# Three buffers of 16 rows, and loads and stores in two parts of every second partition

## The chip, the cores and the metric

The kernel runs on one core of a Trainium2 chip. The metric is device time in microseconds (us), lower is better. A time is the median of the timed executions. The profiled executions give, beside the time, a trace and its span from the first to the last recorded work; the time lies above the span of the same execution (318.93 against 317.3 for the kernel before).

## The reference

Each of 16,384 rows of 1,024 float32 is divided by the sum of its absolute values:

```python
batch, seq, dim = 32, 512, 1024
sums = np.sum(np.abs(x), axis=-1, keepdims=True)
return (x / (sums + 1e-8)).astype(np.float32)
```

67.11 MB have to come in and 67.11 MB have to go out, whatever the kernel does.

## The kernel before

128 partitions (P) take 128 rows at a time in float32. Four buffers hold 12 such rows each, a run of 48 KiB per partition. One DMA loads a buffer, DVE (the vector engine) sums and multiplies, ACT (the scalar engine) multiplies one row (five in the first tile, none in the last four), one DMA stores it. The last tile has 8 rows.

```python
R = 12
BUFS = 4
...
with tc.manual_schedule():
    for i, k in enumerate(rows):          # 12, 12, ..., 12, 8
        x_tile = sbuf.tile([P, R, d], FP32)
        nc.sync.dma_start(out=x_tile[:, :k, :], in_=piece(x_flat, i))
        if i == 0:
            normalize(x_tile, 0, k, k - 5)
        else:
            normalize(x_tile, 0, k, k - 1 if i + BUFS < len(rows) else k)
        nc.scalar.dma_start(out=piece(out_flat, i), in_=x_tile[:, :k, :])
```

`normalize` is a `tensor_reduce` (sum of absolute values), an add of EPS, a reciprocal and a `tensor_mul` on DVE, and for the rows left over a scaled copy each on ACT.

Of the kernel before, what the change touches and what calls it, by code (L numbers as in the profile page):

```python
# [1 line left out]

# [4 lines left out]

FP32 = mybir.dt.float32
EPS = 1e-8


@with_exitstack
def kernel(
    ctx: ExitStack,
    tc: tile.TileContext,
    x: bass.AP,
    out: bass.AP,
):
    nc = tc.nc
    P = nc.NUM_PARTITIONS  # L20

    x_flat = x.flatten_outer_dims()
    out_flat = out.flatten_outer_dims()
    n, d = x_flat.shape




    R = 12
    BUFS = 4  # L30
    HEAD = 32
    per_partition = n // P
    assert n % P == 0 and (per_partition - HEAD) % R == 0
    rows = [R] * ((per_partition - HEAD) // R + 2) + [HEAD - 2 * R]

    def piece(flat, i):
        head = flat[: P * HEAD, :].rearrange("(p r) d -> p r d", p=P)
        if i < 2:
            return head[:, R * i : R * (i + 1), :]
        if i == len(rows) - 1:  # L40
            return head[:, 2 * R :, :]
        a = P * (HEAD + R * (i - 2))
        return flat[a : a + P * R, :].rearrange("(p r) d -> p r d", p=P)

    sbuf = ctx.enter_context(tc.tile_pool(name="sbuf", bufs=BUFS))
    stats = ctx.enter_context(tc.tile_pool(name="stats", bufs=4))

    def normalize(x_tile, r0, k, kv):

        s = stats.tile([P, R], FP32)  # L50
        nc.vector.tensor_reduce(  # L51
            out=s[:, :k],
            in_=x_tile[:, r0 : r0 + k, :],
            axis=mybir.AxisListType.X,
            op=mybir.AluOpType.add,
            apply_absolute_value=True,
        )
        nc.vector.tensor_scalar_add(out=s[:, :k], in0=s[:, :k], scalar1=EPS)  # L58
        inv = stats.tile([P, R], FP32)
        nc.vector.reciprocal(out=inv[:, :k], in_=s[:, :k])  # L60
        nc.vector.tensor_mul(  # L61
            out=x_tile[:, r0 : r0 + kv, :],
            in0=x_tile[:, r0 : r0 + kv, :],
            in1=inv[:, :kv].unsqueeze(2).to_broadcast([P, kv, d]),
        )
        for r in range(kv, k):
            row = x_tile[:, r0 + r, :]
            nc.scalar.activation(  # L68
                out=row,
                in_=row,  # L70
                func=mybir.ActivationFunctionType.Copy,
                scale=inv[:, r : r + 1],
            )

    with tc.manual_schedule():
        for i, k in enumerate(rows):
            x_tile = sbuf.tile([P, R, d], FP32)
            nc.sync.dma_start(out=x_tile[:, :k, :], in_=piece(x_flat, i))  # L78


            if i == 0:
                normalize(x_tile, 0, k, k - 5)
            else:
                normalize(x_tile, 0, k, k - 1 if i + BUFS < len(rows) else k)
            nc.scalar.dma_start(out=piece(out_flat, i), in_=x_tile[:, :k, :])  # L85


# [1 line left out]
_INS = ['x']  # L89
_OUTS = [((32, 512, 1024), 'float32')]  # L90


# [23 lines left out]
```

## Time and profile before

| | before |
|---|---|
| time, median of 3 | 317.25 us (317.13 to 317.62) |
| the profiled execution: time, span | 318.93 us, 317.3 us |
| DVE busy | 268.7 us (85%) |
| ACT busy | 13.5 us (4%) |
| the two DMA queues, share of 16 engines | 49.6% and 48.9% |

The queues' shares add to 98.5%.

### The profile page before, as it was taken

What the parts mean: (1) busy time and instruction counts of PE and PEld (TensorE: products, weight loads), DVE (VectorE), ACT (ScalarE), POOL (GpSimd) and SP (SyncE); (2) the same over time, 40 slices, a digit from 0 to 9 for tenths busy, and PEclk for the clock granted to TensorE, in tenths of its full rate; (3) what the DMA queues carried; (4) which work ended last, traced back from release to release, by engine and by line L of the source; (5) the groups of instructions that cost most, each with busy time, mean ns of one, the idle gap of its engine ahead of it and who ended that gap; (6) DMA issues with size and microseconds to landing.
All of it is one profiled execution on the core that took longest, in us unless ns stands there. A gap on an engine that the chain in (4) does not pass through costs nothing.

```text
span 317.3 us, 170 instructions
## 1 busy us (share of the span) xinstructions
DVE 268.7 (85%) x44; ACT 13.5 (4%) x12; POOL 0.2 (0%) x4
## 2 busy tenths in 40 slices
DVE  0079999999999999989995996799699969999920
ACT  0010601001000000100100010000000000000000
POOL 0000000000000000000000000000000000000000
DMA  8999999999999999999999999999999999999994
GB/s 328 465 397 471 421 378 415 415 465 409 459 434 397 477 415 415 465 409 459 428 403 477 409 428 452 409 471 415 403 477 415 428 430 452 397 477 415 403 425 215
DMA packets 3168, 134.22 MB, mean 423 GB/s; under 512 B 352, under 2 KB 352, under 8 KB 352
## 3 DMA queue, kind: packets, MB, share of 16 engines
q1 hardware_dynamic: 1584, 67.11, 49.6%
q10 hardware_dynamic: 1584, 67.11, 48.9%
HBM read 67.11 MB, written 67.11 MB: 423 GB/s over the span
## 4 chain that ended last, share of the span: by engine, by line
DVE 52%; DMA 34%; another core or an unknown queue 9%; issue 0%; SPq 0%; DVEq 0%; ACTq 0%
DVE s L51 27%; DVE x_tile L61 24%; DMA x_tile<-in_x_dram 18%; DMA out_dram<-x_tile 16%; DVE inv L60 1%; DVE s L58 0%; SPq L78 0%; DVEq L60 0%; ACTq L85 0%
## 5 line engine op out<-in xcount | busy, mean ns | idle before, releaser
L51 DVE TENSOR_REDUCE s<-x_tile 128x12 f32<-128x12288 f32 (+1 forms) x11 | 138.2, 12561 | 32.9 <-DMA x_tile<-in_x_dram 32.9
L61 DVE TENSOR_TENSOR x_tile<-x_tile,inv 128x11264 f32<-128x11264 f32 (+3 forms) x11 | 126.5, 11504 | 0.4
L68 ACT ACTIVATE x_tile<-x_tile,inv 128x1024 f32<-128x1024 f32 x11 | 12.2, 1142 | 153.6 <-DVE inv L60 153.6
L60 DVE RECIPROCAL inv<-s 128x12 f32<-128x12 f32 (+1 forms) x11 | 2.5, 226 | 0.9
L58 DVE TENSOR_SCALAR s<-s 128x12 f32<-128x12 f32 (+1 forms) x11 | 1.9, 173 | 0.4
L68 ACT ACT_TABLE_LOAD x1 | 1.3, 1283 | 17.8 <-DMA x_tile<-in_x_dram 17.8
L100 POOL MEMSET const-bfloat16-1.0<- 128x1 bf16 x1 | 0.1, 102 | 0.0
L100 POOL MEMSET const-uint8-127<- 128x1 uint8 x1 | 0.1, 102 | 0.0
L100 POOL MEMSET const-float32-0.0<- 128x1 f32 x1 | 0.1, 99 | 0.2 <-issue 0.2
L100 POOL MEMSET const-float32-1.0<- 128x1 f32 x1 | 0.1, 99 | 0.0
## 6 DMA issues: line engine op xcount, KB each, us to landing
x_tile<-in_x_dram SPq DMA_DIRECT2D x10, 6144.0 KB, 39.2
out_dram<-x_tile ACTq DMA_DIRECT2D x10, 6144.0 KB, 43.7
x_tile<-in_x_dram SPq DMA_DIRECT2D x1, 4096.0 KB, 35.4
out_dram<-x_tile ACTq DMA_DIRECT2D x1, 4096.0 KB, 13.0
```

The source lines that it names most:

```text
L51: nc.vector.tensor_reduce(out=s[:, :k], in_=x_tile[:, r0 : r0 + k, :], axis=mybir.AxisListType.X, op=mybir.AluOpType.add, apply_absolute_v ...
L58: nc.vector.tensor_scalar_add(out=s[:, :k], in0=s[:, :k], scalar1=EPS)
L60: nc.vector.reciprocal(out=inv[:, :k], in_=s[:, :k])
L61: nc.vector.tensor_mul(out=x_tile[:, r0 : r0 + kv, :], in0=x_tile[:, r0 : r0 + kv, :], in1=inv[:, :kv].unsqueeze(2).to_broadcast([P, kv, d]),)
L68: nc.scalar.activation(out=row, in_=row, func=mybir.ActivationFunctionType.Copy, scale=inv[:, r : r + 1],)
L100: nc = _bacc.Bacc("TRN2", target_bir_lowering=False, num_devices=1)
```

## The change

Its intent is to keep the engines fed with fewer, larger tiles: 3 x 16 rows use the same 48 rows of memory, and splitting each transfer by partition parity lets the even partitions of a buffer be loaded while its odd ones are still stored. DVE gives rows to ACT, and the last tile is finished in two halves of rows. The diff is abridged:

```diff
-    R = 12
-    BUFS = 4
+    R = 16
+    BUFS = 3
+    PARTS = 2
 ...
+        for r in range(k - ka, k):          # ka rows are summed by ACT
+            nc.scalar.activation(out=junk[:, :], in_=rows[:, r, :],
+                func=mybir.ActivationFunctionType.Abs, accum_out=s[:, r : r + 1])
 ...
-            nc.sync.dma_start(out=x_tile[:, :k, :], in_=piece(x_flat, i))
+            for j in range(PARTS):
+                nc.sync.dma_start(
+                    out=x_tile[j::PARTS, :, :], in_=piece(x_flat, i)[j::PARTS, :, :])
+            if i + 1 < tiles:
+                if i == 0:
+                    normalize(x_tile, 5, 6)      # rows summed, multiplied by ACT
+                else:
+                    normalize(x_tile, 0, 3)
+                for j in range(PARTS):
+                    nc.scalar.dma_start(
+                        out=piece(out_flat, i)[j::PARTS, :, :], in_=x_tile[j::PARTS, :, :])
+            else:
+                for h in (slice(0, R // 2), slice(R // 2, R)):
+                    normalize(x_tile[:, h, :], 3, 4)
+                    nc.scalar.dma_start(out=piece(out_flat, i)[:, h, :], in_=x_tile[:, h, :])
```

More of the change, by code (lines that the diff above doesn't have):

```diff
@@ L24, with normalize @@
     n, d = x_flat.shape
-    R = 12
-    BUFS = 4
-    HEAD = 32
-    per_partition = n // P
-    assert n % P == 0 and (per_partition - HEAD) % R == 0
-    rows = [R] * ((per_partition - HEAD) // R + 2) + [HEAD - 2 * R]
-    def piece(flat, i):
-        head = flat[: P * HEAD, :].rearrange("(p r) d -> p r d", p=P)
-        if i < 2:
-            return head[:, R * i : R * (i + 1), :]
-        if i == len(rows) - 1:
-            return head[:, 2 * R :, :]
-        a = P * (HEAD + R * (i - 2))
+    R = 16
+    BUFS = 3
+    PARTS = 2
+    tiles = n // (P * R)
+    assert n == P * R * tiles
+    def piece(flat, i):
+        a = P * R * i
         return flat[a : a + P * R, :].rearrange("(p r) d -> p r d", p=P)
-    sbuf = ctx.enter_context(tc.tile_pool(name="sbuf", bufs=BUFS))
+    sbuf = ctx.enter_context(tc.tile_pool(name="sbuf", bufs=1))
     stats = ctx.enter_context(tc.tile_pool(name="stats", bufs=4))
-    def normalize(x_tile, r0, k, kv):
+    psum = ctx.enter_context(
+        tc.tile_pool(name="psum", bufs=1, space=bass.MemoryType.PSUM)
+    )
+    junk = psum.tile([P, d], FP32)
+    buffers = [sbuf.tile([P, R, d], FP32, name=f"x{b}") for b in range(BUFS)]
+    def normalize(rows, ka, km):
+        k = rows.shape[1]
         s = stats.tile([P, R], FP32)
         nc.vector.tensor_reduce(
-            out=s[:, :k],
-            in_=x_tile[:, r0 : r0 + k, :],
+            out=s[:, : k - ka],
+            in_=rows[:, : k - ka, :],
             axis=mybir.AxisListType.X,
@@ L57, in normalize @@
         )
+        for r in range(k - ka, k):
+            nc.scalar.activation(
+                out=junk[:, :],
+                in_=rows[:, r, :],
+                func=mybir.ActivationFunctionType.Abs,
+                accum_out=s[:, r : r + 1],
+            )
         nc.vector.tensor_scalar_add(out=s[:, :k], in0=s[:, :k], scalar1=EPS)
@@ L61, in normalize @@
         nc.vector.tensor_mul(
-            out=x_tile[:, r0 : r0 + kv, :],
-            in0=x_tile[:, r0 : r0 + kv, :],
-            in1=inv[:, :kv].unsqueeze(2).to_broadcast([P, kv, d]),
-        )
-        for r in range(kv, k):
-            row = x_tile[:, r0 + r, :]
+            out=rows[:, : k - km, :],
+            in0=rows[:, : k - km, :],
+            in1=inv[:, : k - km].unsqueeze(2).to_broadcast([P, k - km, d]),
+        )
+        for r in range(k - km, k):
             nc.scalar.activation(
-                out=row,
-                in_=row,
+                out=rows[:, r, :],
+                in_=rows[:, r, :],
                 func=mybir.ActivationFunctionType.Copy,
@@ L75 @@
     with tc.manual_schedule():
-        for i, k in enumerate(rows):
-            x_tile = sbuf.tile([P, R, d], FP32)
-            nc.sync.dma_start(out=x_tile[:, :k, :], in_=piece(x_flat, i))
-            if i == 0:
-                normalize(x_tile, 0, k, k - 5)
-            else:
-                normalize(x_tile, 0, k, k - 1 if i + BUFS < len(rows) else k)
-            nc.scalar.dma_start(out=piece(out_flat, i), in_=x_tile[:, :k, :])
+        for i in range(tiles):
+            x_tile = buffers[i % BUFS]
+            for j in range(PARTS):
+                nc.sync.dma_start(
+                    out=x_tile[j::PARTS, :, :], in_=piece(x_flat, i)[j::PARTS, :, :]
+                )
+            if i + 1 < tiles:
[5 more added lines that the diff above has]
+                    nc.scalar.dma_start(
+                        out=piece(out_flat, i)[j::PARTS, :, :],
+                        in_=x_tile[j::PARTS, :, :],
+                    )
+            else:
+                for h in (slice(0, R // 2), slice(R // 2, R)):
+                    normalize(x_tile[:, h, :], 3, 4)
+                    nc.scalar.dma_start(
+                        out=piece(out_flat, i)[:, h, :], in_=x_tile[:, h, :]
+                    )
 _INS = ['x']
```

## The prediction

> **What bounds the kernel now.** I began with the busy line and the memory lines of the page. The memory lines carry 67.11 MB in and 67.11 MB out, and the two queues together keep the 16 DMA engines at work 98.5% of the span.
>
> ```profile
> span 317.3 us, 170 instructions
> ...
> DVE 268.7 (85%) x44; ACT 13.5 (4%) x12; POOL 0.2 (0%) x4
> ...
> q1 hardware_dynamic: 1584, 67.11, 49.6%
> q10 hardware_dynamic: 1584, 67.11, 48.9%
> HBM read 67.11 MB, written 67.11 MB: 423 GB/s over the span
> ```
>
> The reader is to see two engines near their limit, DVE at 85% and DMA at 98.5%, and only one of them can be the bound. So next I read the busy time by stretches, with the core's DMA share and GB/s in the last two columns.
>
> ```profile
> 0.00:20.00 20.00, 2.25 (x1) 1.28 (x1) 0.20 (x4) 1.00 0.94 393
> 20.00:40.00 20.00, 19.90 (x5) 5.30 (x5) 0.00 (x0) 1.00 1.00 433
> ...
> 160.00:180.00 20.00, 16.28 (x2) 0.00 (x0) 0.00 (x0) 1.00 1.00 433
> 180.00:200.00 20.00, 15.52 (x5) 1.15 (x1) 0.00 (x0) 1.00 1.00 433
> ...
> 300.00:308.00 8.00, 3.17 (x1) 0.00 (x0) 0.00 (x0) 1.00 0.89 381
> 308.00:317.30 9.30, 0.00 (x0) 0.00 (x0) 0.00 (x0) 1.00 0.56 240
> ```
>
> The rate is the same 433 GB/s where DVE is full (20 to 40 us) and where it rests a fifth of the time (160 to 200 us). The fourteen 20-us stretches from 20 to 300 us lie between 413 and 437 and average 432.6. A share of 1.00 with DVE idle says that the transfers are the bound, and the waits agree: DVE waits for loads, and the load queue waits for stores to free a buffer.
>
> ```profile
> DVE s L51 <- DMA x_tile<-in_x_dram: 32.9, 6, 17.8
> ...
> SPq L78 <- DMA out_dram<-x_tile: 227.0, 7, 55.5
> ```
>
> 17.8 of those 32.9 us are the first load; the other 15.1 us are five waits of 1.1 to 4.3 us between 140 and 259 us. The chain of waits gives DVE 52%, but it runs back along an engine that had slack, so I don't take that share for a bound.
>
> The account of the span follows: 134.22 MB at 432.6 GB/s is 310.3 us. The first 20 us run at 393, which loses (432.6 - 393) x 20 / 432.6 = 1.8 us. From 300 to 308 us it is 381, a loss of 0.95 us: the last multiply ends at 294.48 + 8.69 = 303.17, and the store before the last has about drained by then (the stretch 303 to 304 us has a share of 0.23). From 308 to the end it is 240, a loss of 4.1 us, in which the last packets end unevenly and the last write is confirmed. Sum 310.3 + 1.8 + 0.95 + 4.1 = 317.2.
>
> [...]
>
> **The change part by part.**
> *Bytes:* none removed, none added. The floor of 310.3 us stays. The transfers become 16 loads of 4.19 MB, 14 such stores and two last ones, 32 instead of 22. They queue behind one another, so their issue (0.33 us each on the queue) lies beside transfers already running. A partition's run grows from 48 to 64 KiB; at an unchanged rate I book nothing for it.
>
> *DVE:* a reduce of 12 rows is 12.95 us and of 8 rows 8.68, so 1.07 a row; the multiply of 11 rows is 11.89 and of 7 rows 7.63, also 1.07 a row. The two small operations with their gaps are 0.5 us (30.70 to 31.21). Tile 0: 11 rows reduced 11.9 + 0.5 + 10 rows multiplied 10.8 = 23.2 us. Tiles 1 to 6: 16 rows 17.2 + 0.5 + 13 rows 14.0 = 31.7 us each. Last tile, two halves of 5.5 + 0.5 + 4.4 = 10.4 us. Sum 23.2 + 190.2 + 20.8 = 234 us, 34 us less than 268.7. All of it comes off an engine that isn't the bound, so I value it at nothing in the middle.
>
> *ACT:* 43 row operations instead of 11. At 1.15 us each that is about 50 us, never over 7 us in a row, against 11 to 14 us of DVE beside it (in the last tile 3 x 1.15 and 4 x 1.15 beside 5.5 and 4.4, so at most a few tenths stick out). I take a row sum by ACT to cost what a row copy does.
>
> *Buffers:* 3 x 16 and 4 x 12 are both 48 rows, so as much is loaded before the first store as before: 25.2 MB. Does either queue ever run dry? Tile 0 (8.39 MB) is there at 2 + 8.39 / 0.4326 = about 22 us, normalised at 22 + 23.2 = 45, when 18.8 MB are loaded and 6.4 are left. From then loads and stores share the engines, 216 GB/s each, 19.4 us for a half-buffer transfer. The first half-store lands at 65, with 6.4 - 4.2 = 2.2 MB of loads still queued (10 us of work), and then the next load is released. Every later half repeats this with period 19.4, so loads don't run dry. Stores of tile i are through at about 46 + 38.8 (i + 1); tile 3 is loaded at 114 and normalised at 146, while the stores before it last until 163, a margin of 17 us that repeats because 31.7 is below 38.8. So neither queue runs dry in the middle. Even if a half had to wait for both stores of its buffer, the engines would work off the other queue meanwhile.
>
> *The end:* at 45 us, 67.1 - 18.8 = 48.3 MB are left to load; at 216 GB/s that takes 223 us, so the last load lands near 269. By then 48.3 MB are stored and 18.8 are left, 43 us at full rate. The last tile's halves are ready at 279 and 290. The backlog ahead of them, 18.8 - 8.4 = 10.4 MB, lasts 24 us, until 293. So the last store joins a queue still busy, by some 3 us, and the 0.95 us lost at 300 to 308 us before should go.
>
> *Sum:* 310.3 + 1.8 + 4.1 = 316.2, and as the third loss may return in part or longer runs may save a few tenths, **316.0 us**.
>
> **The rivals.** (1) **Strided halves slow the engines down.** [...] Against it: loads and stores are mixed most of the time,[...] and the row counts of the change look tuned around transfers at full rate. A rate 5% lower means 310.3 x 1.053 + 5.9 = 333 us[...]. I give it one in ten. (2) **A wait for a buffer takes the place of the finer rotation.** Three buffers must carry load, 31.7 us of compute and store within 3 x 38.8 = 116 us. With undivided transfers that is 38.8 + 31.7 + 38.8 = 109, seven to spare; with halves overlapping, one 19.4 less. The margins above speak against it; it could cost 1 to 4 us if completion of halves came late. (3) **The end gets worse:** if the last load lands over 3 us later than I reckon, the last half-store of 4.19 MB stands alone and the lost microsecond stays, 317 to 319. (4) **A real gain from less compute:** only if DVE were the bound. The stretches with a full DMA share and an idle DVE speak against it, and even a loss-free run is 310.3 us plus start and end, about 313; over 2% faster (below 310.9) would need a rate that the engines never show.
>
> **Range and chances.** 313.8 is the floor with some of the end saved; 320 holds rivals 2 and 3. Faster by over 2%: 0.02. Within 2%: 0.87. Slower: 0.11, nearly all of it rival 1.
>
> **What would show it.** Right: both queues' shares still sum to 98 to 99%, the stretches from 20 to 290 us read 430 to 437 GB/s, DVE falls to about 234 us (75% or less) with longer waits for loads, and no dip before the last store. Wrong: a rate under 425 in the load-only first 45 us (rival 1), stretches with the share under 0.97 in the middle (rival 2), or a dip between 285 and 310 us (rival 3). The prediction fails most simply if 64 strided partitions are not spread like 128 whole ones.

Cuts are marked in the text above: passages about the DMA engines and the memory that no trace or run of this case shows, among them a limit for the rate, grounds for and against rival 1, and a loss worked out from them. Rival 1, with its one in ten, is the author's estimate: the kernel before has only transfers of 128 partitions, so no trace then on hand showed one of 64. 310.3 + 1.8 + 4.1 = 316.2 us are worked out from the trace of the kernel before. Only the step from there to the 316.0 us given, for longer runs, is a guess; the traces show no such gain (64 KiB in 2.418 us and 48 KiB in 1.815 are both 27.1 GB/s).

## More of the kernel before

The profiled execution is 1.7 us slower than the median of the timed ones. The stretches at its end, one us each, with the DMA share and GB/s in the last two columns, say why:

```profile
312.00:313.00 1.00, 0.00 (x0) 0.00 (x0) 0.00 (x0) 1.00 1.22 524
313.00:314.00 1.00, 0.00 (x0) 0.00 (x0) 0.00 (x0) 1.00 0.23 98
314.00:315.00 1.00, 0.00 (x0) 0.00 (x0) 0.00 (x0) 1.00 0.08 33
```

A packet is counted where it starts, so a share may exceed 1. The reader is to see that after 313 us only a few packets start: 33 GB/s is one 32 KiB packet in a microsecond. Most of the 16 DMA engines (the engines meant from here on, where no other is named) are done; one still works.

## The result, and the profile after

The changed kernel takes 320.46 us (median of 6, 319.21 to 321.20), the kernel before 316.97 us (median of 6, 316.56 to 317.62). The ratio is 1.0106, 95% interval 1.0081 to 1.013. Ratios here are the mean time of one kernel's fast runs over that of the other's in the same rounds, so not quite the ratio of the medians. The change is clear and small, within 2%, and the time is 0.46 us above the predicted range. It went the wrong way: 0.4% faster was expected (316.0 against 317.25), 1.1% slower came.

The page of the changed kernel, its busy and memory lines (q1 carries the loads, q10 the stores):

```profile
span 319.0 us, 211 instructions
...
DVE 233.5 (73%) x36; ACT 48.2 (15%) x55; POOL 0.2 (0%) x4
...
q1 hardware_dynamic: 1280, 67.11, 49.3%
q10 hardware_dynamic: 1408, 67.11, 48.6%
HBM read 67.11 MB, written 67.11 MB: 421 GB/s over the span
```

DVE lost 35 us and the span grew: compute is not what the kernel waits for. Its waits, and its stretches:

```profile
DVE s L52 <- DMA x<-in_x_dram: 58.6, 6, 23.0
```

```profile
0.00:20.00 20.00, 0.00 (x0) 0.00 (x0) 0.20 (x4) 1.00 0.96 400
20.00:40.00 20.00, 16.82 (x4) 11.53 (x16) 0.00 (x0) 1.00 1.01 439
...
240.00:260.00 20.00, 19.90 (x4) 3.23 (x3) 0.00 (x0) 1.00 1.01 436
260.00:280.00 20.00, 11.67 (x5) 5.04 (x8) 0.00 (x0) 1.00 1.03 446
280.00:300.00 20.00, 13.03 (x5) 10.38 (x13) 0.00 (x0) 1.00 0.94 408
300.00:308.00 8.00, 0.00 (x0) 0.00 (x0) 0.00 (x0) 1.00 1.00 430
308.00:319.00 11.00, 0.00 (x0) 0.00 (x0) 0.00 (x0) 1.00 0.48 209
```

The DMA share lies between 0.94 and 1.07 up to 308 us, and the dip of the kernel before (381 GB/s from 300 to 308) has become 430. The scatter of the stretches, 408 to 459 GB/s from 20 to 300 us, is in the counting: the engines start their 64 KiB packets nearly together, and each packet counts where it starts. With the bytes of each packet spread over its duration, every stretch from 20 to 300 us reads 430 to 434, but for 414 from 40 to 60, where the first store begins. What is lost against the kernel before is lost in the last line. The same end in steps of one us:

```profile
312.00:313.00 1.00, 0.00 (x0) 0.00 (x0) 0.00 (x0) 1.00 0.76 328
313.00:314.00 1.00, 0.00 (x0) 0.00 (x0) 0.00 (x0) 1.00 0.23 98
314.00:315.00 1.00, 0.00 (x0) 0.00 (x0) 0.00 (x0) 1.00 0.08 33
315.00:316.00 1.00, 0.00 (x0) 0.00 (x0) 0.00 (x0) 1.00 0.08 33
316.00:317.00 1.00, 0.00 (x0) 0.00 (x0) 0.00 (x0) 1.00 0.08 33
```

For three microseconds one packet starts per microsecond. The transfers are done but for one engine's share.

**Looking at single engines.** No view names the 16 engines, but the trace records each packet with queue, start, duration and size. One engine's packets follow one another with their records meeting to about 4 ns, so I chained them into 16 sequences. Each has 8.39 MB, to better than 0.1, in the first traces of both kernels. Where two engines are in step a packet may land in the wrong sequence (some sums in other traces are off by more, by 0.5 MB in f4), so I use the ends and averages over all 16, and single packets only where the sequences are well apart.

In the changed kernel most sequences end between 313.0 and 313.8 us, two at 314.6 and 314.8, and one at 317.9. In the kernel before most end at 313.8 to 313.9, two at 314.5 and 315.0 and one at 315.9. Nothing is slow about the packets as such: a 64 KiB packet takes 2.418 us and a 48 KiB one 1.815, both 27.1 GB/s. The late engine has single packets that take longer. Here it is beside an ordinary engine, at the border between two loads (queue: L load, S store; start us, duration ns, bytes; the packets of 4 bytes come at the end of a transfer, 16 to each: 352 for the 22 transfers of the kernel before, 512 for the 32 of the changed one):

```
late engine                     ordinary engine
S 130.13 2418 65536             S 129.57 2418 65536
L 132.54    9     4             L 131.99    9     4
S 132.55 2418 65536             S 131.99 2418 65536
L 134.96 2894 65536             L 134.41 2418 65536
S 137.85 2418 65536             S 136.82 2418 65536
L 140.26 2536 65536             L 139.24 2418 65536
```

It enters 0.56 us late and leaves 1.02 us late. No other sequence has a lengthened packet there. From 115 us on this repeats, mostly at the first packet of a new load, for about 4 us in total. At borders from 194 us on, up to three engines have such a packet at the same time.

### The profile page after: what moved, and what is told of

It is laid out like the page before. It is cut to its first block, busy times and chain, and to the rows that moved or that the text cites. A ratio compares the mean times of both kernels' runs of the same rounds, so it can differ in the third digit from the quotient of the medians.

```text
span 319.0 us, 211 instructions
## 1 busy us (share of the span) xinstructions
DVE 233.5 (73%) x36; ACT 48.2 (15%) x55; POOL 0.2 (0%) x4
## 4 chain that ended last, share of the span: by engine, by line
DMA 51%; DVE 29%; another core or an unknown queue 6%; issue 5%; SPq 0%; ACT 0%; ACTq 0%; DVEq 0%
DMA out_dram<-x 29%; DMA x<-in_x_dram 23%; DVE s L52 18%; DVE x L69 10%; DVE inv L68 0%; SPq L86 0%; ACT x L75 0%; DVE s L66 0%; ACTq L95 0%; DVEq L52 0%; DVEq L66 0%
## 5 line engine op out<-in xcount | busy, mean ns | idle before, releaser
L52 DVE TENSOR_REDUCE s<-x 128x16 f32<-128x16384 f32 (+2 forms) x9 | 126.2, 14018 | 58.6 <-DMA x<-in_x_dram 58.6
L69 DVE TENSOR_TENSOR x<-x,inv 128x13312 f32<-128x13312 f32 (+2 forms) x9 | 103.8, 11536 | 0.3
L75 ACT ACTIVATE x<-x,inv 128x1024 f32<-128x1024 f32 x32 | 34.2, 1137 | 202.1 <-DVE inv L68 202.1
L60 ACT ACTIVATE junk<-x 128x1024 f32<-128x1024 f32 x11 | 11.3, 1027 | 19.8 <-DMA x<-in_x_dram 18.9
L68 DVE RECIPROCAL inv<-s 128x16 f32<-128x16 f32 (+1 forms) x9 | 2.2, 242 | 0.3
L60 ACT ACTIVATION_READ_ACCUMULATOR junk<-x 128x1 f32 x11 | 2.0, 186 | 0.0
L66 DVE TENSOR_SCALAR s<-s 128x16 f32<-128x16 f32 (+1 forms) x9 | 1.6, 174 | 0.5
```

The costliest lines, as they stand in the source:

```text
L52: nc.vector.tensor_reduce(out=s[:, : k - ka], in_=rows[:, : k - ka, :], axis=mybir.AxisListType.X, op=mybir.AluOpType.add, apply_absolute_ ...
L60: nc.scalar.activation(out=junk[:, :], in_=rows[:, r, :], func=mybir.ActivationFunctionType.Abs, accum_out=s[:, r : r + 1],)
L66: nc.vector.tensor_scalar_add(out=s[:, :k], in0=s[:, :k], scalar1=EPS)
L68: nc.vector.reciprocal(out=inv[:, :k], in_=s[:, :k])
L69: nc.vector.tensor_mul(out=rows[:, : k - km, :], in0=rows[:, : k - km, :], in1=inv[:, : k - km].unsqueeze(2).to_broadcast([P, k - km, d]),)
L75: nc.scalar.activation(out=rows[:, r, :], in_=rows[:, r, :], func=mybir.ActivationFunctionType.Copy, scale=inv[:, r : r + 1],)
```

## The experiments

Seventeen kernels ran, in five groups; each group's chip also ran the kernel before. The table has what the traces say of the engines: when the median and the last engine finished its last packet, and by how much an engine's packets were longer than the usual duration of their size, summed and averaged over the engines.

| run | median us (range) | before, same chip | ratio [95%] | median / last engine ends | lengthened us |
|---|---|---|---|---|---|
| before, first trace | | | | 313.9 / 315.9 | 2.3 |
| changed, first trace | 320.46 (319.21–321.20) | 316.97 | 1.0106 [1.0081, 1.013] | 313.4 / 317.9 | 2.3 |
| e1 whole transfers | 319.24 (318.81–320.12) | 317.11 | 1.0061 [1.0027, 1.0095] | 315.9 / 316.7 | 4.9 |
| e2 before, strided halves | 319.19 (318.27–319.70) | 317.11 | 1.0055 [1.0021, 1.0089] | 313.7 / 316.1 | 2.2 |
| e3 halves cut by rows | 316.82 (316.65–317.16) | 317.11 | 0.9984 [0.9952, 1.0016] | 313.4 / 313.9 | 1.7 |
| changed, again | 320.83 (316.79–324.38) | 317.11 | 1.0063 [1.0008, 1.0119] | 313.4 / 321.4 | 2.3 |
| f1 8 rows, strided halves | 317.55 (317.40–318.14) | 317.69 | 0.9988 [0.9947, 1.0029] | 313.8 / 315.2 | 1.6 |
| f2 8 rows, whole | 317.15 (316.91–317.81) | 317.69 | 0.9976 [0.9934, 1.0017] | 313.3 / 313.9 | 1.5 |
| f3 halves 0–63, 64–127 | 477.78 (471.23–481.07) | 317.69 | 1.4901 [1.4773, 1.5029] | 463.7 / 478.1 | |
| f4 strided quarters | 359.23 (352.51–361.11) | 317.69 | none given | 350.9 / 357.6 | 22.3 |
| g1 f2 + given lag | 330.99 (324.16–337.94) | 316.92 | 1.0243 [1.0207, 1.0278] | 322.1 / 322.2 | 2.9 |
| g2 f1 + given lag | 321.24 (320.91–321.42) | 316.92 | 1.013 [1.0107, 1.0152] | 316.9 / 317.7 | 3.2 |
| g3 halves in, whole out | 330.62 (328.24–332.52) | 316.92 | 1.0419 [1.0376, 1.0461] | 327.5 / 328.5 | 10.7 |
| g4 before, last tile halved | 317.27 (317.00–322.19) | 316.92 | 1.0007 [0.9984, 1.003] | 313.4 / 314.0 | 2.0 |
| h1 e1, short sums | 325.90 (322.95–330.08) | 317.02 | 1.0187 [1.0167, 1.0206] | 316.9 / 320.6 | 6.4 |
| h2 changed, short sums | 320.33 (319.90–320.74) | 317.02 | 1.0104 [1.0089, 1.0119] | 313.5 / 317.8 | 2.9 |
| h3 strided, 32 KiB runs | 330.13 (326.04–331.92) | 317.02 | 1.0362 [1.0318, 1.0405] | 324.0 / 328.4 | 11.3 |
| i1 before, again | 317.26 (316.48–319.24) | 316.85 | 0.9991 [0.994, 1.0043] | 313.1 / 314.1 | 2.0 |
| i2 e3 again | 316.98 (316.62–317.56) | 316.85 | 0.9974 [0.9921, 1.0026] | 313.5 / 314.6 | 1.8 |

A run counts as slow when it is over 1.5% above the fastest run of the same kernel; the granted clock was 1.0 in all. The medians in the table are of all runs, the ratios of fast ones alone. Where they differ much, the fast runs were: changed again, four at 316.79 to 320.89; f3, 471.23 and 476.49; f4, 352.51 alone; g1, 324.16 and 325.40; h1, three at 322.95 to 323.62; h3, four at 326.04 to 330.35. Where it matters, differences below are taken from these. The profiled executions of "changed, again", f3, f4 and h3 are slow by that rule; what is read from those of f3, f4 and h3 is there in their fast times as well, and the first trace of the changed kernel is a fast one.

### First group: number of transfers, length of runs, or the stride

Theory A: every border between transfers costs the late engine something, and there are 32 transfers instead of 22. Theory B: a run of 64 KiB makes a bigger lag. Theory C: the strided halves make it.

**e1**, the changed kernel with whole transfers:

```diff
-    PARTS = 2
+    PARTS = 1
```

> The changed kernel with every load and store whole again (one DMA of 128 partitions x 64 KiB). In the trace of the changed kernel 15 of the 16 DMA engines appear to be done by about 313.7 us and the work after that comes one 32 KiB packet at a time (stretches of 0.08 DMA share from 314 to 317 us): one engine is late. Theory A, the late engine loses a few tenths of a us at the borders between transfers, so their number counts: 17 transfers instead of 32, so 316 to 317.5 us. Theory B, the 64 KiB runs make one engine's lag larger: stays at 319.5 to 321 us. Theory C, the strided half-partition transfers do it: 316 to 317.5 us, as under A.

It took 319.24 us, between the theories, and the trace shows why: no late engine (the last ends 0.8 us after the median), but every engine is later. At the borders from 156 us on both queues run dry: a store waits for the multiply, and a load waits for a whole store. The first packet of the store that starts then takes longer, on 14 or 15 of the 16 engines. One of them, as above:

```
L 155.81 2418 65536
L 158.21    9     4
S 158.22 3256 65536
S 161.47 2418 65536
```

The store was issued at 156.4 us, when the engines had ended the store before it at 155.6 to 156.5 (one at 158.3). The packet is 0.84 us longer; the same was there near 198 and 276 us, and half of it near 237, together about 3 us on most engines. I first put this down to the restart of the load queue (a load was issued at 158.7 us), and the expectation of g3 below still does. The trace says otherwise: at 276 us no load is issued any more (the last was at 237.4), and at 85.5 us, where the load queue starts again beside busy stores after 12 us without a packet, no packet is longer. So releasing halves does earn something, which the prediction had put at nothing. The test of A, B and C itself came out open here.

**e2**, the kernel before with strided halves, 44 transfers of 48 KiB runs:

```diff
-            nc.sync.dma_start(out=x_tile[:, :k, :], in_=piece(x_flat, i))
+            for j in range(2):
+                nc.sync.dma_start(out=x_tile[j::2, :k, :], in_=piece(x_flat, i)[j::2, :, :])
```

and the stores likewise.

> The kernel before (four buffers of 12 rows, 48 KiB runs) with each load and store as two DMAs of every second partition, nothing else changed: 44 transfers instead of 22. Theory A (number of transfers) and theory C (strided halves): slower than before by 2 to 5 us, 319 to 322 us, with a late engine at the end. Theory B (64 KiB runs): no slower than before, 316.5 to 317.5 us.

319.19 us, 2.1 above before on the same chip, with a late engine at 316.1. Its end reads as expected of A and C:

```profile
313.00:314.00 1.00, 0.00 (x0) 0.00 (x0) 0.00 (x0) 1.00 0.23 98
314.00:315.00 1.00, 0.00 (x0) 0.00 (x0) 0.00 (x0) 1.00 0.08 33
```

**e3**, the changed kernel with its two parts cut by rows: each transfer has 128 partitions and 8 rows.

```diff
-    out=x_tile[j::PARTS, :, :], in_=piece(x_flat, i)[j::PARTS, :, :]
+    out=x_tile[:, 8 * j : 8 * j + 8, :], in_=piece(x_flat, i)[:, 8 * j : 8 * j + 8, :],
```

and the stores likewise.

> The changed kernel with its two DMAs cut by rows instead of partitions: each is 128 partitions x 8 rows, a run of 32 KiB; number of transfers, release by halves and compute as in the changed kernel. Theory A (number of transfers): stays at 319.5 to 321 us. Theory B (64 KiB runs) and theory C (strided halves): falls to 315.5 to 317.5 us.

316.82 us, and all 16 engines end between 313.3 and 313.9. Its end:

```profile
311.00:312.00 1.00, 0.00 (x0) 0.00 (x0) 0.00 (x0) 1.00 0.68 295
312.00:313.00 1.00, 0.00 (x0) 0.00 (x0) 0.00 (x0) 1.00 1.21 524
313.00:314.00 1.00, 0.00 (x0) 0.00 (x0) 0.00 (x0) 1.00 0.01 0
```

The last packets start together and nothing follows. Buffers, compute, the number of transfers and the release by halves are those of the changed kernel. Theory A falls. In this rotation the strided cut, with the 64 KiB runs that come with it, is what costs some 2.6 to 3.6 us (fast runs of the changed kernel average 319.38 us in this group, and the result's median was 320.46). e2 had the strided cut without the longer runs, so theory B alone doesn't do either.

**The changed kernel again:**

> The changed kernel again, for a second trace and the spread: 319.2 to 321.2 us; if one late engine is the cause, the stretches after 314 us again show a DMA share of 0.04 to 0.1 for 2 to 4 us; if the tail of the first trace was chance, they don't, and the time falls with it.

320.83 us, with runs from 316.79 to 324.38. Its trace is of the slowest run: the median engine ends at 313.4 us as in the first trace, and one ends at 321.4. So these two executions differ by their late engine. One of the six runs, at 316.79, is as fast as the kernel before: the late engine is frequent with this cut, not certain.

### Second group: stride at 32 KiB, and other cuts

**f1 and f2** have six buffers of 8 rows (32 KiB runs), f1 with strided halves, f2 with whole transfers. The diff of f2 from the changed kernel, with the row counts for ACT scaled down and the last tile stored at once:

```diff
-    R = 16
-    BUFS = 3
-    PARTS = 2
+    R = 8
+    BUFS = 6
+    PARTS = 1      # f1 keeps 2
```

> Six buffers of 8 rows (32 KiB runs) with each load and store as two DMAs of every second partition (62 transfers or so). Cutting by rows removed the late engine at 32 KiB runs, so it is open whether the strided cut or the long run makes it. Theory C (strided half-partition transfers make one engine late): at least 2 us slower than the same kernel with whole transfers that goes with it, 319 to 323 us, late engine at the end. Theory B (long runs): the same as that kernel to 0.7 us, both 315.5 to 317.5 us.

> Six buffers of 8 rows, every load and store one DMA of 128 partitions x 32 KiB: the control of the strided one. Both theories: no late engine, 315.5 to 317.5 us, like the row-cut kernel (316.8).

317.55 against 317.15 us. The strided one has an engine 1.5 us after the median, the whole one 0.6. With 32 KiB runs the stride costs some 0.4 us, hardly clear of the spread; with 48 KiB it had cost 2.1 (e2). That looked like theory B on top of C: a slip of one packet, and longer packets, longer slips.

**f3 and f4** keep the changed kernel and cut it otherwise: partitions 0 to 63 and 64 to 127, and every fourth partition.

```diff
-    x_tile[j::PARTS, :, :]
+    x_tile[64 * j : 64 * j + 64, :, :]      # f3
-    PARTS = 2
+    PARTS = 4                               # f4
```

> The changed kernel with its two halves as partitions 0 to 63 and 64 to 127 instead of every second one; 64 KiB runs, same number of transfers. Rival 1 of the prediction[...]: loads alone run at half the rate in the first 45 us, the first reduce starts near 40 us instead of 23, and the total is over 340 us. [...]

> The changed kernel with four DMAs of every fourth partition for each load and store (32 partitions, 64 KiB runs, twice as many transfers). If each start of a strided transfer costs the late engine a few tenths of a us, the tail doubles: 322 to 328 us. If a strided transfer costs nothing by itself and only the run's length counts: 319 to 321 us, as the changed kernel.

f3 took 477.78 us. While it only loads, in its first 40 us:

```profile
0.00:20.00 20.00, 0.00 (x0) 0.00 (x0) 0.20 (x4) 1.00 1.01 210
20.00:40.00 20.00, 0.00 (x0) 0.00 (x0) 0.00 (x0) 1.00 1.02 210
```

The engines are busy throughout (share 1.01) and move half: 64 KiB packets of 5.118 us instead of 2.418. So it matters which 64 partitions a transfer covers: the changed kernel, with every second one, reads 439 GB/s from 20 to 40 us. Why, no run here tells. The expectation had carried rival 1 over to this cut; half the rate and a total of over 340 us came as it said, with tile 0 there at 44.1 us (near 40). f4 took 359.23 us, 352.51 in its only fast run, much worse than expected by either theory. Its load-only stretch from 20 to 40 us still has 436 GB/s; the rate falls later, to 379 from 140 to 200 us and 368 from 200 to 260, with the share at 0.96 to 0.98, because packets get longer.

### Third group: a lag given on purpose

f4 suggested a phase theory, a guess until then: strided parts run freely while all engines are in step, and slow one another when one is not. To test it, two engines were to get 1.8 us more work than the others, early, in the whole (g1) and in the strided (g2) kernel with 8 rows:

```diff
+            if i == 2:
+                for j in range(4):
+                    nc.sync.dma_start(out=scratch[2 * j : 2 * j + 2, :],
+                        in_=x_flat[: 6, :].rearrange("(p r) d -> p (r d)", p=2))
```

> The kernel with six buffers of 8 rows and whole transfers (317.15 us, no late engine), with four extra loads of 2 partitions x 12 KiB into a scratch tile, queued behind the loads of tile 2: they should give one or two DMA engines about 48 KiB, 1.8 us, more work than the others. All theories: the late engines keep the lag they were given and no more, 318.4 to 319.2 us (1.3 to 2.0 above its twin without the extra loads).

> The same extra loads in the twin with every second partition (317.55 us, two engines 1 us late). Phase theory:[...] no two engines meet as long as all are in step, but an engine out of step meets another one and both lose; so a lag that is given grows: over 3 us above its twin, 320.5 to 330 us, and other engines are slowed too. Rival (a strided transfer costs one engine time whether it is in step or not): the given lag only adds, 318.8 to 319.6 us.

g1 missed. The whole one lost some 8 us by its two fast runs (324.16 and 325.40 against 317.15 in the second group), where 1.3 to 2.0 had been expected. The strided one lost 3.7 (321.24 against 317.55), within what the phase theory had said of it, but the whole one should then have lost less, and it lost more. Eight packets of 12 KiB appear in the trace of g1, 0.46 us each, so the work given is as planned. The lag it makes is larger than planned: on the two engines each extra load packet takes turns with a 32 KiB store packet, and the next load ends on them at 63.2 us, on the others near 55. By the chained sequences they are about 1 us of work behind at 60 us and 4.2 at 290: they keep losing a few tenths at nearly every border. The last load ends near 288 us on the others and at 299.4 and 300.5 on these two, and the other 14 engines stand idle for some 5 us near 295 and 3 near 309, as the stores of the last two tiles can't start before:

```profile
285.00:290.00 5.00, 5.00 (x1) 0.00 (x0) 0.00 (x0) 1.00 1.00 433
290.00:295.00 5.00, 4.83 (x4) 1.15 (x1) 0.00 (x0) 1.00 0.77 334
295.00:300.00 5.00, 3.39 (x1) 0.00 (x0) 0.00 (x0) 1.00 0.34 144
```

Most of the loss is this waiting, 7.3 us per engine on average. A lag therefore grows in whole-partition transfers too; the stride isn't needed for that. In g2 nearly all engines stood idle for 1.1 to 1.7 us near 42 us and started again together, after which they kept close (0.8 us of tail).

**g3**, loads in strided halves, stores whole, to see whether the restarts of e1 put engines in step:

```diff
-                for j in range(PARTS):
-                    nc.scalar.dma_start(
-                        out=piece(out_flat, i)[j::PARTS, :, :], in_=x_tile[j::PARTS, :, :])
+                nc.scalar.dma_start(out=piece(out_flat, i), in_=x_tile[:, :, :])
```

> The changed kernel with loads still as two DMAs of every second partition, but each store one whole DMA, so both halves of a load wait for the whole store. The kernel with whole transfers (319.24 us) showed the load queue running dry at each tile, and the packet in flight at each restart 0.8 us longer on all 16 engines, four times. Phase theory: the restart puts the engines in step again, so the late engine goes (under 1.5 us of tail) and 318.5 to 320 us remain from the restarts. Rival (strided loads cost time in or out of step): restarts and late engine add up, 321 to 324 us.

330.62 us, worse than both expectations. Packets on all engines are longer, 10.7 us per engine. Mixing two cuts is worse here than either alone (whole 319.24 us, strided halves 320.46). The phase theory as I had put it, with engines meeting because of the stride, falls.

**g4**, the kernel before with the last tile in two halves:

```diff
+            elif i + 1 == len(rows):
+                h = k // 2
+                for r0 in (0, h):
+                    normalize(x_tile, r0, h, h - 2)
+                    nc.scalar.dma_start(out=piece(out_flat, i)[:, r0 : r0 + h, :],
+                        in_=x_tile[:, r0 : r0 + h, :])
+                continue
```

> The kernel before with one part of the change alone: its last tile of 8 rows normalised and stored in two halves of 4 rows, two of the rows of each multiplied by ACT. In the trace of before nearly all engines wait 0.3 to 0.9 us near 303 us for the last multiply. If that dip is worth its size: 0.3 to 0.9 us faster than before; if the engines' unevenness takes its place: within 0.3 us of before.

317.27 us, ratio 1.0007. The dip before the last store is worth nothing measurable; a second trace of the kernel before, in the fifth group, doesn't have it.

### Fourth group: stride and run length apart

At 64 KiB stride and whole had not been compared without dry queues. Sums over a quarter of each row (wrong results) shorten DVE's work (the sums of all tiles take 32.6 us instead of 126.2) so that stores are ready in time:

```diff
-            in_=rows[:, : k - ka, :],
+            in_=rows[:, : k - ka, : d // 4],
```

> Wrong sums on purpose: the kernel with whole 64 KiB transfers (319.24 us, queue restarts at every tile), with each sum over a quarter of its row, so DVE has 13 us less per tile and stores are ready before the queue is dry. Strided theory (every second partition brings the first engine out of step): no restarts and no late engine, 314.5 to 316.5 us. Run-length theory (64 KiB runs alone make a slip of 2.4 us that grows): a late engine for whole transfers too, 318 to 324 us.

> The changed kernel with the same short sums (wrong on purpose), the control: strided halves, 64 KiB runs. Both theories: late engine remains, as compute isn't part of it, 319 to 324 us. If it falls to 317 us, the sums' length matters, and neither theory is complete.

The whole one takes 325.90 us (323.2 as the mean of its fast runs), the strided one 320.33. So whole 64 KiB transfers have late engines as well, five that end at 319.6 to 320.6 us, and here the strided ones are the better of the two. The test is not quite clean: near 87 us the load queue of h1 still ran dry once (its loads had ended at 81.9 to 86.8 us, the next was issued at 87.4). The stretch from 48 to 80 us of h1:

```profile
48.00:80.00 32.00, 12.95 (x1) 2.15 (x3) 0.00 (x0) 1.00 0.99 381
```

Share 0.99 and 381 GB/s: busy engines, longer packets. In the packet records two groups of engines alternate load and store in opposite phase there, and both groups' packets are 0.3 to 1.1 us longer.

**h3**, the changed kernel with each strided half cut again by rows: four transfers, 32 KiB runs, same stride, buffers and compute.

```diff
             for j in range(PARTS):
-                nc.sync.dma_start(
-                    out=x_tile[j::PARTS, :, :], in_=piece(x_flat, i)[j::PARTS, :, :])
+                for h in (slice(0, R // 2), slice(R // 2, R)):
+                    nc.sync.dma_start(
+                        out=x_tile[j::PARTS, h, :], in_=piece(x_flat, i)[j::PARTS, h, :])
```

and the stores likewise.

> The changed kernel with each strided half cut again by rows: four DMAs of 64 strided partitions x 8 rows, runs of 32 KiB, same buffers, compute and release. Run-length theory (given the stride, the slip is one run long): the late engine loses most of its lag, 317 to 318.2 us. If stride alone counts: 319.5 to 322 us as the changed kernel; if the number of strided transfers counts, over 322.

330.13 us, 326.04 to 330.35 in its fast runs. Shorter runs didn't help, it got worse: engines end anywhere from 319.4 to 328.4. The run-length theory falls too, as far as one edit can show it that also doubles the number of strided transfers. That number isn't the answer by itself either: f1 has 64 strided transfers with 32 KiB runs and takes 317.55 us, h3 has 60 and takes over 326. What differs is the rotation, six buffers of 8 rows against three of 16, and with it when transfers are issued.

### Fifth group: is the kernel before in step?

Its only trace was of an execution 1.7 us over the median.

> The kernel before, unchanged, for a second trace: its first trace (317.3 us span, a run of 318.9 us) had one engine 2 us late, but its timed runs have a median of 317 us, and times lie some 1.7 us over the span. If the typical run has no late engine: span 315 to 315.6 us, no stretch after 314 us with DMA work. If the late engine of 2 us is typical: span 317 us and a time of 318.8 us, above the other runs.

> The kernel with its halves cut by rows again, for a second comparison with the kernel before: if it is in step every time, 316.5 to 317.2 us with all runs within 0.7 us, and 0.1 to 0.5 us below before; if its first result was luck, some runs over 318 us.

The second trace of the kernel before has a span of 315.5 us (time 317.15) and ends like this:

```profile
300.00:308.00 8.00, 0.65 (x1) 0.00 (x0) 0.00 (x0) 1.00 0.87 377
...
311.00:312.00 1.00, 0.00 (x0) 0.00 (x0) 0.00 (x0) 1.00 1.06 459
312.00:313.00 1.00, 0.00 (x0) 0.00 (x0) 0.00 (x0) 1.00 0.38 164
313.00:314.00 1.00, 0.00 (x0) 0.00 (x0) 0.00 (x0) 1.00 0.01 0
```

No straggler: the last engine ends at 314.1 us. So the typical execution of the kernel before is in step, as far as one trace and the times show, with some of its runs at 319 to 321 us. The dip isn't there either: the last multiply ends at 300.65 us, 2.5 us earlier than in the first trace, and no engine idles, where 13 had idled 0.3 to 0.9 us near 303.5 in the first. (That the stretch reads 377 is the counting of packets where they start.) The row-cut kernel was again at 316.98 us, 316.62 to 317.56; over both groups its twelve runs stay under 317.6. It equals the kernel before and doesn't beat it: both ratios' intervals contain 1. No version here beats the kernel before by a clear margin.

## Why the prediction was wrong

The range was 313.8 to 320.0 us, the measured median 320.46.

**What held.** The bound: 134.22 MB at the rate of 16 engines, with DVE's 35 us worth nothing. DVE came to 233.5 us (234 predicted), ACT to 48.2 (about 50), waits for loads grew from 32.9 to 58.6 us, the packet rate did not change (64 KiB in 2.418 us, 48 KiB in 1.815), so rival 1 as a general slowdown was rightly set aside. The queues' shares sum to 97.9%, and the stretches read 430 to 437 GB/s only with the bytes spread over the packets' durations. The schedule: tile 0 was there at 23.0 us (22), its multiply done at 46.3 (45), the last load there at 272.4 (269), the last halves ready at 282.9 and 293.3 (279 and 290). Issuing took longer than the 0.33 us reckoned with: 0.47 us at the median for the load of a half, 0.58 for its store, and up to 2.8 for a store.

**What failed: the end in the sum**, that is, the 4.1 in "310.3 + 1.8 + 4.1 = 316.2" and the 0.95 us left out of it. The 4.1 us of uneven end were copied from the trace of the kernel before as if they were a fixed cost. They are not fixed. They contained one late engine, which the second trace of that kernel doesn't have (last engine at 314.1 instead of 315.9 us), and the changed kernel has a later one (317.9). From 308 us to the end, 11 us at 209 GB/s lose 11 x (432.6 - 209) / 432.6 = 5.7 us instead of 4.1. With the bytes of each packet spread over its duration it is 5.2 us, against 3.2 in the first trace of the kernel before and 2.2 in its second. From 20 to 300 us the two kernels hardly differ: 431.7 GB/s in the changed one and 431.5 in the kernel before, reckoned in this way.

The gain at the end failed as well. The dip, 0.95 us, was left out of the new sum as something that the change would save, but a typical execution of the kernel before doesn't have it (i1), and halving the last tile alone saves nothing (g4).

A second slip is mine alone: the sum is a span and was given as a time. A span of 316.0 is a time of about 317.7. So of the 4.5 us between 316.0 and 320.46, some 1.7 are this. Of the other 2.7 about 2 are the later end of the last engine (317.9 instead of 315.9), and most of the rest is the dip's gain that brought no earlier end. That the sum for the kernel before, 317.2, met its median time of 317.25 was luck: it is the span of an execution that took 318.93.

The 3.5 us between the two kernels are found the same way. In the second trace of the kernel before the last engine ends at 314.1 us and the span 1.4 us later; in the changed kernel at 317.9 and 1.1 later: 3.8 - 0.3 = 3.5 us of span, as the medians have it. The median engine ends at 313.1 and at 313.4. Nearly the whole difference is one engine.

**Rival 2** was mis-sized in its ground: "Even if a half had to wait for both stores of its buffer, the engines would work off the other queue meanwhile." They do while that queue has work; where both had run dry, the first packet of the next store was up to 0.8 us longer on nearly all engines. e1 shows 4.9 us of lengthening per engine where e3 has 1.7, and it is 2.4 us slower in the same group; the "1 to 4 us" of the rival had the right size for it. With halves the load queue did not run dry in the first trace, but its margin was thin: when a load was issued, the queue's earlier packets lasted another 1.2 to 4.7 us, not the 10 us that I had counted on.

**What is shown and what stays open.** Shown: the changed kernel loses its time through a late DMA engine. Cutting by rows instead of by partitions, with the same buffers, compute, number of transfers and release (e3), removes it (two traces with a tail of 0.5 and 1.2 us, and twelve times that all stay under 317.6 us). This also halves the runs, but the strided cut makes the kernel before slower too, with its runs as they were (e2). A lag given to two engines grows also without stride (g1: from 1 us of work at 60 us to 4.2 at 290).

Not shown: what makes an engine fall behind and lose at the borders. No simple answer fits all runs. It isn't the number of transfers (e3 has as many and is in step). It isn't the stride alone (h1 has none and is worse than h2), nor the length of the runs alone (h3 has short ones and is worse, f1 has the same and isn't). Nor is it only the stride that makes engines out of step lose (in g1 the lag grows without it). Packets do get longer with the engines busy: by 0.3 to 1.1 us in h1, in engines that load while others store, and from 2.418 to 5.118 us in f3. That engines out of step slow one another is a guess from this; no run here shows whether they do, or where.

## What to carry to other kernels

Here the two queues kept the 16 DMA engines busy for 98.5% of the span before and 97.9% after, and the last engine set the time: in the changed kernel it ended 4.5 us after the median one (317.9 against 313.4), and nearly all of the 3.5 us lost are this. In a kernel bound like this one, read the last microseconds in steps of one, and don't carry a tail or a dip over from one trace of one execution. Check first whether that execution's time is a typical one. Where whole transfers let the queues run dry, as in e1, a release by halves was worth 2.4 us (e3, 316.82 against 319.24). But try the halves cut by rows over all 128 partitions before those cut by partitions: here they gave the same overlap with all engines in step (all end between 313.3 and 313.9 us in e3), and 316.82 against 320.46 us. And compare a profiled span with a time only after adding what lies outside the span, 1.6 to 2.2 us here.
